# Score passes of a sliding-window attention: the keys' low parts of two head pairs in one matmul

## The chip, the cores and the metric

The kernel runs on one core of one Trainium2 chip. A core has TensorE (matmuls, called PE in the profile, its weight loads PEld), VectorE (DVE), ScalarE (ACT), GpSimd (POOL) and SyncE (SP), which here does nothing but issue DMAs. Each engine works through its own instructions in order and waits on semaphores for the others. The metric is the device time of one execution in microseconds; less is better.

## The reference

One layer of a hybrid decoder block on x of 2048 positions by 1024 channels, all in float32. What matters here is the attention branch: 16 query heads and 4 key/value heads of 64 channels, a window of 128 positions, QK-norm and a sink per head.

```
h = rms_norm(x, norm_g)
u = jnp.einsum('bsd,dc->bsc', h, w_in)      # v_c, b_c, c_c, z_c, q, k, v, z_a, gate_logits
y_a = einsum(b_c * causal_depthwise_conv(c_c * v_c, conv_w) * silu(z_c), w_conv_out)
scores = jnp.einsum('bnqhgd,bnkhd->bnhgqk', qb, kb) * scale     # blocks of 128 queries, 256 keys
p = softmax with sinks over the valid keys (0 <= q_pos - k_pos < 128)
o = einsum(p, vb) * silu(z_a)
y_b = einsum(o, w_attn_out)
out = x + einsum(sigmoid(gates_a) * y_a + sigmoid(gates_b) * y_b, w_out)
```

A position sees itself and the 127 before it, so a block of 64 queries needs 192 keys.

## The kernel before, in words

**Numbers.** TensorE takes float32 operands of a rounded kind (float32r). To keep float32 accuracy every operand is split into a high part (rounded) and a low part (what is left), and a product is a sum of passes: high times high, high times low, low times high.

**Stages.** The sequence is worked through in two tiles of 1024 positions (`t`). In each, "units" run one after the other: k, v, q, the convolution's columns (`cv`, `b`), the gates (`ga`, `gb`), `za`, `z`, and then `ya` and `yb`; at the end of both the output projection `o`. A unit `S` has seven products of 12 passes of 512 columns (`product`, L368). The generators yield after each product, and each yield is a tick: in `run` a tick calls `ahead_loads` (weight loads), then one `piece` of the preparation of the next unit's weights, and whatever was put down for that tick with `put`. The order of every engine is written out in this way; no scheduler changes it.

**Weights.** `load_half` (L246 for the units `S`) brings one half of a unit's raw weights into a tile of `rawpool` with two DMAs on SyncE, up to two units ahead. A unit's pieces then form sums and differences of the raw halves and split them: the pieces "a", "d", sums, "s" and "t", each with a high part copied by ACT (L273) and a low part subtracted by DVE (L274, into tiles called w..al, w..d, w..sl, w..tl). "s" is the last to read the second half, "t" the last to read the first. A raw tile is used again when its last reader has ended, and the DMA that fills it waits for that on SyncE.

**Attention.** While these units run, attention goes along in their ticks: 32 steps for each `t`, one for each key/value head `j` and block `b` of 128 positions (`attention`; the first 16 at every 5.25 ticks, the others at every 3.25). For a step at tick n:

- n - 4: `att_load` brings queries and keys from DRAM: `q2` (L713), for each of the two halves h (64 queries each) and the two head pairs c a 128x128 tile, with the high parts of 64 channels in partitions 0 to 63 and the low parts in 64 to 127; `k2` (L718; L720 and L722 in the first block of a tile), the keys' high parts and low parts of 256 positions, each stored twice over, in partitions 0 to 63 and again in 64 to 127.
- n: `att_scores`. A score tile takes two PSUM banks, one for each h. For each h and c there are two passes (L752) with the weights `q2[:, h, c]`: with the keys' high parts and with the keys' low parts, 192 columns each. Eight passes in all; a pass over the low parts adds low times low as well. The first block of the sequence has 64 or 128 columns, as it has no earlier keys. DVE then masks and takes the maximum (L758 to L764) and forms the biases.
- n + 1: ACT takes the exponentials (`att_exp`, L777); value tiles are loaded (`att_load_v`, L734 and L739).
- n + 2 to n + 8: DVE normalizes, TensorE transposes (L793), ACT, DVE and POOL split and mask (L796 to L806), TensorE multiplies with the values (L823, six passes of 256 columns), ACT and DVE join the halves (`att_out`), and SyncE stores the result to `od` (L836).

There is one score tile (`ps_s`), so a block's scores wait for the exponentials of the block before.

**Queues.** All loads and stores named so far, and the gates' stores (L897), are issued by SyncE, in the program's order: one that waits holds up all behind it. SyncE's transfers take turns with eight semaphores, so that each also waits for the landing of the one eight places ahead of it. POOL's own queue writes the queries, keys and values to DRAM (L609, L698).

Of the kernel before, what the change touches and what calls it, by code (L numbers as in the profile page):

```python
# [8 lines left out]
F32 = mybir.dt.float32  # L9
F32R = mybir.dt.float32r  # L10
# [5 lines left out]
P = 128  # L16
D = 1024
KC = D // P
T = 1024
H = 512  # L20
HB = H // P
NB = T // P
# [3 lines left out]
HD = 64  # L26
# [12 lines left out]
LH, UH = slice(0, HD), slice(HD, P)  # L39
HALVES = (LH, UH)  # L40
# [3 lines left out]
def block_kernel(  # L44
# [15 lines left out]
    nc = tc.nc  # L60
# [5 lines left out]
    consts = ctx.enter_context(tc.tile_pool(name="consts", bufs=1))  # L66
    oppool = ctx.enter_context(tc.tile_pool(name="oppool", bufs=28))
    wpool = ctx.enter_context(tc.tile_pool(name="wpool", bufs=8))
    rawpool = ctx.enter_context(tc.tile_pool(name="rawpool", bufs=5))
    big = ctx.enter_context(tc.tile_pool(name="big", bufs=19))  # L70
    upool = ctx.enter_context(tc.tile_pool(name="upool", bufs=2))
    small = ctx.enter_context(tc.tile_pool(name="small", bufs=12))
# [6 lines left out]
    def slot(shape, dt, name):  # L79
        return big.tile(shape, dt, tag="big", name=name)  # L80
# [7 lines left out]
    def mbank(name):  # L88
# [8 lines left out]
    q2d = [[dram.tile([P, 2 * NB, 2, 2, HD], F32, name=f"q2d{t}_{j}") for j in range(NKV)]  # L97
           for t in range(NT)]
    kd = [dram.tile([NKV, P, 2, T], F32, name=f"kd{t}") for t in range(NT)]
# [113 lines left out]
    def add(o, a, b, eng=None):  # L213
        return (eng or nc.vector).tensor_tensor(out=o, in0=a, in1=b, op=ALU.add)  # L214
# [4 lines left out]
    def mul(o, a, b, eng=None):  # L219
        return (eng or nc.vector).tensor_tensor(out=o, in0=a, in1=b, op=ALU.mult)  # L220


    plan, raws, ready, used, todo = [], {}, [], [0], []
    WRING, RAWS = 8, 5
    live, rawlive = [0], [0]

    def load_half(i=None, first=None):
# [478 lines left out]

    def att_load(t, j, b):
        nm = f"{t}_{j}_{b}"  # L710
        gb = t * NB + b
        q2 = slot([P, 2, 2, P], F32R, f"q2_{nm}")
        nc.sync.dma_start(  # L713
            q2.bitcast(F32).rearrange("p h c x -> p (h c x)"),
            q2d[t][j][:, 2 * b : 2 * b + 2].rearrange("p h c e x -> p (h c e x)"))
        k2 = slot([P, 2, 2 * P], F32R, f"k2_{nm}")
        if b > 0:
            nc.sync.dma_start(k2.bitcast(F32), kd[t][j, :, :, (b - 1) * P : (b + 1) * P])  # L718
        else:
            nc.sync.dma_start(k2[:, :, P:].bitcast(F32), kd[t][j, :, :, 0:P])  # L720
            if gb > 0:
                nc.sync.dma_start(k2[:, :, :P].bitcast(F32), kd[t - 1][j, :, :, T - P : T])  # L722
        return q2, k2

    def att_load_v(t, j, b):

# [15 lines left out]
    def att_scores(t, j, b, ld):  # L742
        first = t * NB + b == 0
        nm = f"{t}_{j}_{b}"
        q2, k2 = ld
        rv = rqs[t, j][:, b // HB, b % HB]
        sp = ps_s.tile([P, 2, 2, 2 * P], F32, tag="s", name=f"s{nm}")
        for h in range(2):
            skip = (2 - h) * HD if first else 0
            for c in range(2):  # L750
                for l in range(2):
                    nc.tensor.matmul(  # L752
                        sp[:, h, c, skip : 3 * HD], lhsT=q2[:, h, c, :],
                        rhs=k2[:, l, h * HD + skip : h * HD + 3 * HD], start=l == 0, stop=l == 1)
        sg = sp.rearrange("p h c k -> p (h c) k")
        m = mask_i.unsqueeze(1).to_broadcast([P, G, HD])
        if first:
            nc.vector.copy_predicated(  # L758
                sg[:, :, 2 * HD : 3 * HD], m, negc.unsqueeze(1).to_broadcast([P, G, HD]))
            nc.vector.tensor_copy(sg[:, 0:2, HD : 2 * HD], negc.unsqueeze(1).to_broadcast([P, 2, HD]))  # L760
        else:
            nc.vector.copy_predicated(sg[:, :, 2 * HD : 3 * HD], m, sg[:, :, 0:HD])
        st = small.tile([P, 6, G], F32, tag="st", name=f"st{nm}")
        nc.vector.tensor_reduce(out=st[:, 0], in_=sg[:, :, HD : 3 * HD], axis=AX.X, op=ALU.max)  # L764
        mul(st[:, 5].rearrange("p (h c) -> p h c", c=2), st[:, 0].rearrange("p (h c) -> p h c", c=2), rv)
        nc.vector.scalar_tensor_tensor(
            out=st[:, 1], in0=st[:, 5], scalar=-1.0, in1=nsink_r[:, j].rearrange("p h c -> p (h c)"),
            op0=ALU.mult, op1=ALU.min)
        add(st[:, 2], sink_r[:, j].rearrange("p h c -> p (h c)"), st[:, 1])
        return sg, st, rv  # L770
# [314 lines left out]
    for n in range(S // P // 2):  # L1085
        t, c0 = divmod(2 * n * P, T)
# [112 lines left out]
    def attention(t, places):  # L1199
        for r, n in enumerate(places):  # L1200
            j, b = divmod(r, NB)
            got = {}

            def step(k, f, got=got):
                def g():
                    got[k] = f(got)
                return g

            put(n - 4, step("l", lambda g, j=j, b=b: att_load(t, j, b)))
            put(n + 1, step("v", lambda g, j=j, b=b: att_load_v(t, j, b)))  # L1210
            put(n, step("s", lambda g, j=j, b=b: att_scores(t, j, b, g["l"])))
            put(n + 1, step("e", lambda g, j=j, b=b: att_exp(t, j, b, g["s"])))
            put(n + 2, step("n", lambda g: att_norm(g["e"])))
            put(n + 4, step("x", lambda g, j=j, b=b: att_turn(t, j, b, g["n"])))
            put(n + 7, step("o", lambda g, j=j, b=b: att_values(t, j, b, g["x"], g["v"])))
            put(n + 8, step("z", lambda g, j=j, b=b: att_out(t, j, b, g["o"])))
# [139 lines left out]
```

## Time and profile before

| | us |
|---|---|
| median of 3 runs | 2016.96 (2016.4 to 2018.07) |
| the profiled execution | 2018.62 |
| its span | 2016.9 |
| TensorE busy in it | 1998.2 |
| score passes (L752), 512 of them, busy | 67.3 |
| their weight loads, busy | 65.6 |
| SyncE's key loads (L718, L720, L722) | 68 transfers |

The granted clock of TensorE was 0.999 of full speed over the span. Matmuls overlap in the profile, as the next one starts before the last has left the array: what a pass takes is the distance between two starts and not the duration shown for one. In the rows of the timeline a piece is a run of equal instructions: start, length, engine, line, operation, tiles written and read, shape and count. A row of an engine's line (say L718) gives the least, median and greatest duration of one instruction; for a DMA that is the time that its issue takes on SyncE, and "DMA to landing" is the time from the issue's start to the landing of its data. Issues on SyncE include a wait, if their time is much longer than others of the same line.

### The profile page before, as it was taken

How to read it: one execution, taken by the hardware profiler on the slowest of the kernel's cores; microseconds unless marked ns; L12 is line 12 of the kernel's file. 1: busy time of each engine (PE TensorE's matmuls, PEld its weight loads, DVE VectorE, ACT ScalarE, POOL GpSimd, SP SyncE). 2: the span in 40 equal slices, each digit the busy share in tenths (PEclk: the TensorE clock that was granted, in tenths of full speed). 3: DMA queues.
4: the chain of work that ended last, by engine and by line, in shares of the span. 5: the costliest groups of instructions: out<-in, count | busy, mean ns of one | idle time of the engine just before them, and what ended most of it. 6: DMA issues, size and time to landing. Idle time of an engine off the chain costs nothing.

```text
span 2016.9 us, 27508 instructions
## 1 busy us (share of the span) xinstructions
PE 1998.2 (99%) x9488; PEld 1664.3 (83%) x9488; DVE 1381.9 (69%) x2361; ACT 933.9 (46%) x1847; POOL 373.3 (19%) x519
## 2 busy tenths in 40 slices
PE   8999999999999999999999999999999999999999
PEld 6788888888888888888888888888888888888887
DVE  6878888787775565358777887886776656356654
ACT  7554554456564343244555454555665334112321
POOL 1462222123230000000272212212322000100000
PEclk9999999999999999999999999999999999999999
DMA  6484443456464535765485434445556444765553
GB/s 181 126 206 121 131 122 104 123 151 184 149 173 157 193 105 159 237 204 163 119 208 153 121 94 124 132 139 157 168 173 185 145 142 136 250 217 165 172 172 110
DMA packets 315707, 316.18 MB, mean 157 GB/s; under 512 B 21564, under 2 KB 235632, under 8 KB 315568
## 3 DMA queue, kind: packets, MB, share of 16 engines
q1 hardware_dynamic: 302528, 276.37, 45.2%
q0 software_dynamic: 13024, 38.06, 7.3%
q8 instruction: 75, 1.23, 0.3%
q14 instruction: 64, 0.52, 0.1%
q10 hardware_dynamic: 16, 0.00, 0.0%
HBM read 217.61 MB, written 96.73 MB: 156 GB/s over the span
## 4 chain that ended last, share of the span: by engine, by line
PE 88%; DVE 5%; ACT 4%; issue 1%; SPq 1%; DMA 1%; ACTq 0%; DVEq 0%
PE Y L368 28%; PE yb L953 9%; PE ya L953 8%; PE Xcv L368 4%; PE Vcv L368 4%; PE s L752 2%; PE Vb L368 2%; PE Xb L368 2%; PE Xza L368 2%; PE Xo L368 2%; PE Xz L368 2%; PE Vz L368 2%; PE Vza L368 2%; PE Vo L368 2%; PE Vq L368 2%; PE po L823 2%
## 5 line engine op out<-in xcount | busy, mean ns | idle before, releaser
L806 POOL TENSOR_SCALAR_AFFINE_SELECT xh<-xh 64x512 fp32r<-64x512 f32 x64 | 67.6, 1056 | 661.9 <-DVE xl L798 536.1
L777 ACT ACTIVATE p<-s,st,rq 128x128 f32<-128x128 f32 x256 | 113.3, 453 | 0.7
L214 DVE TENSOR_TENSOR o<-po,o 64x256 f32<-64x256 f32 x128 | 53.7, 419 | 59.3 <-ACT o L834 59.2
L987 DVE SCALAR_TENSOR_TENSOR tha<-tha,ya 128x512 f32<-128x512 f32 x32 | 22.0, 687 | 94.3 <-PE ya L953 90.9
L834 ACT COPY o<-po 64x256 f32<-64x256 f32 x128 | 46.9, 367 | 85.0 <-DVE o L214 83.5
L798 DVE TENSOR_TENSOR xl<-pt,xh 128x512 fp32r<-128x512 f32 x64 | 44.2, 690 | 57.3 <-ACT yp L797 53.6
L953 PE MATMUL ya<-opa,wya_1h 128*128 128x512 f32 x256 | 79.7, 391 | 1.0 <-ACT opa L210 0.5
L368 PE MATMUL Xcv<-oph,wcv_ah 128*128 128x512 f32 x256 | 79.7, 393 | 0.0
L953 PE MATMUL yb<-opb,wyb_0h 128*128 128x512 f32 x256 | 79.5, 392 | 0.0
L953 PE MATMUL yb<-opb,wyb_1h 128*128 128x512 f32 x256 | 79.5, 392 | 0.0
L953 PE MATMUL ya<-opa,wya_0h 128*128 128x512 f32 x256 | 78.9, 390 | 0.0
L752 PEld LDWEIGHTS s<-k,q 128*128 128x128 f32 x512 | 65.6, 191 | 8.9 <-ACT p L777 5.3
L210 ACT CAST opb<-ocr 128x512 fp32r<-128x512 f32 x32 | 19.9, 621 | 110.4 <-DMA ocr<-ocd 109.2
L752 PE MATMUL s<-k,q 128*128 128x192 f32 (+2 forms) x512 | 67.3, 274 | 2.7 <-ACT p L777 2.5
L1007 DVE SCALAR_TENSOR_TENSOR thb<-thb,yb 128x512 f32<-128x512 f32 x32 | 21.9, 686 | 55.2 <-PE yb L953 55.2
L953 PEld LDWEIGHTS ya<-opa,wya_1h 128*128 128x128 f32 x256 | 48.1, 188 | 12.3 <-ACT opa L210 1.4
L698 POOL DMA_DIRECT2D vd<-v x32 | 20.2, 637 | 199.6 <-DVE v L211 197.3
L953 PEld LDWEIGHTS ya<-opa,wya_0h 128*128 128x128 f32 x256 | 48.1, 188 | 10.0
L953 PEld LDWEIGHTS yb<-opb,wyb_1h 128*128 128x128 f32 x256 | 47.6, 188 | 9.6
L953 PEld LDWEIGHTS yb<-opb,wyb_0h 128*128 128x128 f32 x256 | 47.6, 188 | 9.6
L368 PEld LDWEIGHTS Xcv<-oph,wcv_ah 128*128 128x128 f32 x256 | 47.0, 188 | 9.0
L806 POOL TENSOR_SCALAR_AFFINE_SELECT yp<-xl 64x512 fp32r<-64x512 f32 x64 | 53.5, 836 | 3.1
(583 smaller groups left out, 6202.8 us busy)
## 6 DMA issues: line engine op xcount, KB each, us to landing
wcv_raw<-in_w_in SPq DMA_DIRECT2D x64, 256.0 KB, 4.3
q<-q2d SPq DMA_DIRECT2D x64, 256.0 KB, 4.0
v<-vd SPq DMA_DIRECT2D x128, 128.0 KB, 3.9
gd<-th SPq DMA_DIRECT2D x64, 256.0 KB, 2.1
k<-kd SPq DMA_DIRECT2D x56, 256.0 KB, 4.3
wq_raw<-in_w_in SPq DMA_DIRECT2D x32, 256.0 KB, 4.4
q2d<-q_h POOLq DMA_DIRECT2D x64, 128.0 KB, 3.9
q2d<-q_l POOLq DMA_DIRECT2D x64, 128.0 KB, 4.1
```

The source lines that it names most:

```text
L214: return (eng or nc.vector).tensor_tensor(out=o, in0=a, in1=b, op=ALU.add)
L368: nc.tensor.matmul(ps, lhsT=w[:, j, :], rhs=b[:, m, :], start=start and j == 0 and i == 0, stop=j == KP - 1 and i == 2, skip_group_check=n ...
L698: nc.gpsimd.dma_start(to, v[half].bitcast(F32).rearrange("p b l d -> p b (l d)"))
L752: nc.tensor.matmul(sp[:, h, c, skip : 3 * HD], lhsT=q2[:, h, c, :], rhs=k2[:, l, h * HD + skip : h * HD + 3 * HD], start=l == 0, stop=l == 1)
L777: nc.scalar.activation(out=p[:, i, :], in_=sg[:, i, HD : 3 * HD], func=AF.Exp, bias=st[:, 1, i : i + 1], scale=rv[:, i // 2, i % 2 : i % 2 ...
L798: nc.vector.tensor_tensor(out=xl, in0=pt, in1=xh.bitcast(F32), op=ALU.subtract)
L806: nc.gpsimd.affine_select(out=d4, in_=s4, pattern=[[0, 2 * G], [-sg, HD]], compare_op=ALU.is_gt if prev else ALU.is_ge, fill=0.0, base=0, ...
L823: nc.tensor.matmul(po[:, cs], lhsT=v2[:, kind, :], rhs=xx.rearrange("p g q -> p (g q)")[:, cs], start=n == 0, stop=n == 2)
L834: nc.scalar.copy(ov, pov[oth, :, :, e, :])
L953: nc.tensor.matmul(ps, lhsT=w[:, j, cs], rhs=o[:, m, :], start=n == 0 and i == 0, stop=n == KC - 1 and i == 2)
L987: nc.vector.scalar_tensor_tensor(out=m, in0=m, scalar=1.0, in1=ps, op0=ALU.add, op1=ALU.mult)
L1007: nc.vector.scalar_tensor_tensor(out=m, in0=m, scalar=1.0, in1=ps, op0=ALU.add, op1=ALU.mult)
```

## The change

The products of the queries' high parts with the keys' low parts are taken for both head pairs of a half in one pass, and low times low is no longer computed. The weights of that pass hold the high parts of the queries of pair 0 in partitions 0 to 63 and of pair 1 in partitions 64 to 127. The moving operand has 384 columns: the low parts of 192 keys in partitions 0 to 63 with zeros under them, and beside them the same keys' low parts in partitions 64 to 127 with zeros above. So each pair meets its keys in its own 192 columns. For each h there are then three passes: one of 384 columns into both pairs' places, and one of 192 for each pair with the weights `q2` as before and the keys' high parts, added to it.

The moving operands with the zeros stand in two lasting tiles, `lows`, used by turns; POOL fills them with zeros once, and loads write only the parts with keys. A second tile, `kq`, takes the place of `k2`: it holds the keys' high parts and the weights of the new pass. `lows` takes 4 KB of each partition; the raw weight tiles are cut from five to four (4 KB each). `att_load` issues six transfers in place of two (in the first block of the second tile nine in place of three). The order of everything else on all engines is the same.

```diff
-    rawpool = ctx.enter_context(tc.tile_pool(name="rawpool", bufs=5))
+    rawpool = ctx.enter_context(tc.tile_pool(name="rawpool", bufs=4))
...
-    WRING, RAWS = 8, 5
+    WRING, RAWS = 8, 4
...
+    lows = [consts.tile([P, 2, 2 * P], F32R, name=f"lows{i}") for i in range(2)]
+    for kz in lows:
+        nc.gpsimd.memset(kz.bitcast(F32), 0.0)
+
     def att_load(t, j, b):
...
+        kz = lows[(j * NB + b) % 2]
         q2 = slot([P, 2, 2, P], F32R, f"q2_{nm}")
...
-        k2 = slot([P, 2, 2 * P], F32R, f"k2_{nm}")
-        if b > 0:
-            nc.sync.dma_start(k2.bitcast(F32), kd[t][j, :, :, (b - 1) * P : (b + 1) * P])
-        else:
-            nc.sync.dma_start(k2[:, :, P:].bitcast(F32), kd[t][j, :, :, 0:P])
-            if gb > 0:
-                nc.sync.dma_start(k2[:, :, :P].bitcast(F32), kd[t - 1][j, :, :, T - P : T])
-        return q2, k2
+        kq = slot([P, 2, 2 * P], F32R, f"kq_{nm}")
+        for c in range(2):
+            nc.sync.dma_start(
+                kq[HALVES[c], 1].bitcast(F32).rearrange("p (h x) -> p h x", h=2),
+                q2d[t][j][LH, 2 * b : 2 * b + 2, c].rearrange("p h e x -> p h (e x)"))
+
+        blocks = [(t, b - 1, 0, 2)] if b else [(t, 0, 1, 1)]
+        if b == 0 and gb > 0:
+            blocks.append((t - 1, NB - 1, 0, 1))
+        for kt, k0, to, n in blocks:
+            here, there = slice(to * P, (to + n) * P), slice(k0 * P, (k0 + n) * P)
+            nc.sync.dma_start(kq[:, 0, here].bitcast(F32), kd[kt][j, :, 0, there])
+            for c in range(2):
+                nc.sync.dma_start(kz[HALVES[c], c, here].bitcast(F32), kd[kt][j, HALVES[c], 1, there])
+        return q2, kq, kz
...
         for h in range(2):
             skip = (2 - h) * HD if first else 0
+            keys = slice(h * HD + skip, (h + 3) * HD)
+            nc.tensor.matmul(
+                sp[:, h, :, skip : 3 * HD], lhsT=kq[:, 1, h * P : (h + 1) * P], rhs=kz[:, :, keys],
+                start=True, stop=False)
             for c in range(2):
-                for l in range(2):
-                    nc.tensor.matmul(
-                        sp[:, h, c, skip : 3 * HD], lhsT=q2[:, h, c, :],
-                        rhs=k2[:, l, h * HD + skip : h * HD + 3 * HD], start=l == 0, stop=l == 1)
+                nc.tensor.matmul(
+                    sp[:, h, c, skip : 3 * HD], lhsT=q2[:, h, c, :], rhs=kq[:, 0, keys],
+                    start=False, stop=c == 1)
```

More of the change, by code (lines that the diff above doesn't have):

```diff
@@ L744, in att_scores @@
         nm = f"{t}_{j}_{b}"
-        q2, k2 = ld
+        q2, kq, kz = ld
         rv = rqs[t, j][:, b // HB, b % HB]
```

## The prediction

> **What bounds the kernel now.** I read the page's shares and its chain first, then the chain of waits over a few microseconds of attention, then the timelines of TensorE and of SyncE's queue around single score blocks.
>
> ```profile
> span 2016.9 us, 27508 instructions
> PE 1998.2 (99%) x9488; PEld 1664.3 (83%) x9488; DVE 1381.9 (69%) x2361; ACT 933.9 (46%) x1847; POOL 373.3 (19%) x519
> PE 88%; DVE 5%; ACT 4%; issue 1%; SPq 1%; DMA 1%; ACTq 0%; DVEq 0%
> ```
>
> TensorE is busy for 99% of the span and carries 88% of the chain. So a shorter pass pays one for one, as long as nothing that TensorE waits for comes later. The prices of passes come from the merged chain (start, length up to the next piece, count) and, for the narrow ones, from the timeline of TensorE:
>
> ```profile
> 435.99 0.23 PE Xga L368
> 436.21 0.87 PE s L752 x8
> 437.08 2.76 PE Y L368 x12
> 439.84 0.71 PE po L823 x6
> 440.55 0.44 PE pt L793 x4
> ...
> 303.83 1.00 PE L752 MATMUL s<-k,q 128*128 128x64 f32 x8
> 304.67 0.69 PE L368 MATMUL Y<-oph,wcv_th 128*128 128x512 f32 x2
> ```
>
> Per pass that is 0.87/8 = 0.109 us at 192 columns, 2.76/12 = 0.230 at 512, 0.71/6 = 0.118 at 256 and 0.44/4 = 0.110 at 128. The last two rows are a first block of a sequence, whose eight passes have 64 and 128 columns: from 303.83 to 304.67 is 0.84 us, or 0.105 each. So from 64 to 192 columns a pass costs the same: what it costs is its weight load, which the next pass must wait for. From 256 on the columns cost. A score block of eight loads is bound by loads, and this is what the change touches.
>
> **The change, part by part.**
>
> *Fewer passes.* Each half of a score block had four passes of 192 columns; it gets one of 384 and two of 192. Columns stay at 768, loads fall from four to three. No 384-column pass is in the trace. Its bounds are the 256-column pass (0.118) and the 512-column one (0.230); it lies halfway, so I take 0.174. A block then costs 2 x 0.174 + 4 x 0.109 = 0.784 us, 0.086 less than 0.87; 60 blocks give 5.2 us. The four first blocks have passes of 128, 64, 64 and 256, 128, 128 columns: 5 x 0.105 + 0.118 = 0.64 against 0.84, 0.8 us for four. The gain is 6.0 us. At the ends it would be 0.20 us a block (12.7 us in all) with 0.118, and with 0.230 a loss of 0.026 us a block, 0.8 us in all after the first blocks' gain.
>
> The Trainium skill, TensorE: Matmul & The Clock Gate, Back-to-back issue gap, gives a warm pass N/2.4 + 2.5 ns; by columns alone, a half would cost 332.5 ns before (four of 192) and 327.5 after, an estimate of no gain (0.6 us in 60 blocks). The rows above speak against that rule here, since 64 and 192 columns cost the same; the same page's LDWEIGHTS section gives P/1.2 ns, 107 for 128 columns, with which the 0.109 agrees.
>
> *More waits on TensorE.* The six loads of a block need more wait instructions: two or three ahead of its first pass, where one or two stood, and one between the 384-column pass and the next. The wait ahead of the block at 436.21 cost nothing (the row before it ends where it starts). I take nothing, as the issuer has 0.17 us of the long pass to cover one; uncovered they would be about 0.05 us a block, 3 us.
>
> *More transfers on SyncE.* A block's q and k transfers become six (nine in place of three where a sequence's tile crosses into the next): q2 as before, two of the queries' high parts (64 partitions), one of the keys' high parts, two of their low parts (64 partitions). What an issue costs and when keys land:
>
> ```profile
> L718 SPq DMA_DIRECT2D k<-kd x56: 532/537/1588, 174.7 to 1505.1; - x56
> L739 SPq DMA_DIRECT2D v<-vd x64: 588/591/1800, 170.9 to 1518.5; - x64
> L713 SPq DMA_DIRECT2D q<-q2d x64: 325/522/1303, 144.3 to 1504.4; - x64
> DMA to landing us min/median/max: 3.1/4.3/6.9
> ```
>
> The last row belongs to the first. By the nearest rows the new five are 2 x 0.55 (between the k and v rows) + 0.52 (q) + 2 x 0.47 (v's first issue at 207.63, below) = 2.56 us in place of 0.54: the last keys of a block are issued 2.0 us later. Bounds: five of 0.33 (the least in the q row), 1.1 us later, and five of 0.59, 2.4 us later. The 64 blocks add some 130 us of issues to a queue that is idle or waiting for most of the attention; they are paid only where keys land late. Everything behind them on SyncE (weights, od, yd and gd stores, value loads) slips as much; weights are loaded a whole unit ahead, seven products of 2.76 us, which covers it.
>
> *Four raw tiles.* At most four are ever live, so what is loaded ahead and the order of work stay the same on every engine; the fifth only spares a wait. Now the first half of a pair is loaded into a spare tile and the second half waits for the last reader of the "s" piece (the DVE subtraction into w..sl). With four tiles the first half waits for that, and the second for the last reader of the "t" piece. SyncE issues in order, so value, query and key loads stand behind that wait. An example, the pair ahead of the block at 219.79 (SyncE, then DVE, then TensorE):
>
> ```profile
> 200.71 6.75 SPq L246 DMA_DIRECT2D wcv_raw<-in_w_in  x4
> 207.63 0.47 SPq L734 DMA_DIRECT2D v<-vd  x1
> 208.16 0.59 SPq L739 DMA_DIRECT2D v<-vd  x1
> 208.86 1.30 SPq L713 DMA_DIRECT2D q<-q2d  x1
> 210.27 0.53 SPq L718 DMA_DIRECT2D k<-kd  x1
> ...
> 205.27 1.22 DVE L274 TENSOR_TENSOR wb_sl<-wb_raw,wb_sh 128x1024 fp32r<-128x1024 f32 x1
> 209.09 1.21 DVE L274 TENSOR_TENSOR wb_tl<-wb_raw,wb_th 128x1024 fp32r<-128x1024 f32 x1
> ...
> 219.79 1.03 PE L752 MATMUL s<-k,q 128*128 128x192 f32 x8
> ```
>
> The wait ends at 209.09 + 1.21 = 210.30 in place of 205.27 + 1.22 = 206.49: 3.8 us later. With 2.0 us of issues the last key transfer starts near 210.27 + 5.8 = 216.1 and lands, by the median 4.3, at 220.4: 0.6 us after its block wants it, where it had 5.2 us to spare. Three other blocks are near the edge:
>
> ```profile
> 526.67 2.24 SPq L246 DMA_DIRECT2D wgb_raw<-in_w_in  x4
> 529.57 0.54 SPq L718 DMA_DIRECT2D k<-kd  x1
> 536.67 1.03 PE L752 MATMUL s<-k,q 128*128 128x192 f32 x8
> ...
> 553.81 0.54 SPq L718 DMA_DIRECT2D k<-kd  x1
> 561.60 1.12 PE L752 MATMUL s<-k,q 128*128 128x192 f32 x8
> ...
> 1280.77 1.37 SPq L718 DMA_DIRECT2D k<-kd  x1
> 1290.68 1.03 PE L752 MATMUL s<-k,q 128*128 128x192 f32 x8
> ```
>
> From issue to use they have 7.1, 7.8 and 9.9 us; less 2.0 for issues and the 4.3 they keep 0.8, 1.5 and 3.6, and a landing of 6.9 makes the first two late by 1.8 and 1.1. I take four such blocks late by 0.6 us each, 2.4 us given back. At the ends none is late, or about every fourth block, 16, is.
>
> *Where TensorE waits for DVE and ACT.* In the dense parts of attention it already does (430 to 600 us, then 1345 to 1525):
>
> ```profile
> PE Vgb L368 <- DVE wgb_sl L274: 1.5, 1, 1.5
> PE s L752 <- ACT p L777: 1.4, 2, 1.2
> ...
> PE pt L793 <- DVE p L220: 1.8, 1, 1.8
> PE s L752 <- ACT p L777: 1.1, 2, 0.7
> ```
>
> There a shorter score block only waits longer. Some 26 blocks lie up to the last of these waits, 26 x 0.086 = 2.2 us; DVE's and ACT's chains themselves start from the scores, so I take a quarter as lost, 0.6 us (bounds 0 and 2.2).
>
> *The memsets.* Two more of POOL's 128x512 fills:
>
> ```profile
> 2.06 0.52 POOL L130 MEMSET zero<- 128x512 f32 x1
> 8.30 0.19 POOL L148 COPY seen<-x 128x1 f32<-128x1 f32 x1 [5.73 <-DMA x<-in_x]
> ```
>
> 1.04 us lies in the 5.73 us in which POOL waits for x: nothing.
>
> **The sum.** -6.0 + 2.4 + 0.6 = -3.0 us. The profiled execution took 2018.62 us, its span and 1.7 us around it, and would be 2015.6; against the runs' median of 2016.96, 1.7 us below it, the forecast is 2014.0 us.
>
> **The rivals.** *The queue decides (slower).* SyncE's lateness, not TensorE, sets the attention. For it: the blocks above, where a key transfer has 0.6 to 3.6 us left, and 6.9 us landings that happen already. Against it: most blocks are not right behind a raw pair. With 16 blocks late by 0.75 us it gives 12 - 6.0 + 0.6 = +6.6, 2023.6 us; it turns the sign from nine blocks of 0.6 us on (5.4 us). *All hidden.* Landings stay near 3.1 to 4.3 us, the small transfers land sooner, and only the 0.6 us is lost: -5.4, 2011.6 us. For it: medians that leave room in all but one of the four blocks. *No gain from TensorE.* The 384-column pass costs as much as 512 (0.230): +0.8, and with the late blocks +2.4 it is 2020.2 us; against it stands the evenly rising price between 256 and 512 columns. The skill page's columns-alone rule is this rival too.
>
> **How the numbers follow.** Forecast 0.42, all hidden 0.18, the queue 0.30, no gain 0.10. Within 0.2% (4.0 us; about what a measurement of this kernel can tell from no change) lies most of the forecast. The side faster by over 4.0 takes all hidden and a third of the forecast (its stalls may be half as long): 0.18 + 0.15 = 0.33. Slower by over 4.0 takes the queue but for a tenth, plus a little of no gain: 0.30. The rest is 0.37. The range: below, all hidden with a slightly cheaper pass, 2010.5; above, the queue rival at its middle and a little over, 2025. The forecast's own range is 2011.5 to 2016.5.
>
> **What would show it.** Of the changed kernel: a full score block (passes at L765 and L769) from first pass to the next product in 0.78 us; the weight loads of the score down from 512 to 384; a block behind a raw pair waiting for kq or lows for about half a microsecond, four or so in all; SyncE's waits at L246 naming w..tl beside w..sl; waits for DVE and ACT in the dense parts slightly longer. Wrong would be: a block of 0.87 us or more (the pass's price), waits for keys in ten blocks and more (the queue), or none at all (all hidden).

## The result and the profile after

The changed kernel takes 2013.72 us (median of 22 runs, 2012.46 to 2015.92), the kernel before 2017.32 (22 runs, 2016.35 to 2019.41): a ratio of 0.9982, 95% interval 0.9976 to 0.9988. The forecast was 2014.0. The time came out nearly as forecast; the working did not.

The profiled execution took 2012.82 us. From its page, first the span and the shares, then the chain by engine:

```profile
span 2011.1 us, 27717 instructions
...
PE 1992.2 (99%) x9360; PEld 1656.5 (82%) x9360; DVE 1383.4 (69%) x2361; ACT 934.0 (46%) x1847; POOL 375.3 (19%) x521
...
PE 90%; DVE 4%; ACT 3%; issue 2%; DMA 1%; POOL 0%; SPq 0%; POOLq 0%; ACTq 0%; DVEq 0%
```

TensorE still bounds the kernel, with 128 matmuls and as many weight loads fewer. The score block whose chain the prediction quoted (436.21 us before) looks like this after, in the merged chain of the same place (start, length, count):

```profile
435.14 0.17 PE s L765
435.31 0.20 PE s L769 x2
435.51 0.20 PE s L765
435.71 0.20 PE s L769 x2
435.91 2.81 PE Y L368 x12
```

The block takes 0.77 us in place of 0.87. But the twelve passes of 512 columns behind it, which the change does not touch, take 2.81 us in place of 2.76. Over the 15 full blocks between 1098 and 1343 us the medians of the block are 0.871 before and 0.766 after, the means of the twelve passes 2.756 and 2.807: 0.105 gained, 0.051 lost again, 0.053 us kept (3.627 to 3.574 for both together). From the thirteenth pass on there is no difference. A first block of a sequence, in TensorE's timeline:

```profile
303.58 0.22 PE L765 MATMUL s<-lows,kq 128*128 128x128 f32 x1
...
304.20 0.68 PE L368 MATMUL Y<-oph,wcv_th 128*128 128x512 f32 x2
```

From 303.58 to 304.20 it takes 0.62 us in place of 0.84. What TensorE waits for (sum, times, longest), rows with scores, transposes and the gates' weights, first before, then after:

```profile
PE s L752 <- ACT p L777: 2.5, 4, 1.2
PE pt L793 <- DVE p L220: 2.2, 2, 1.8
...
PE Vgb L368 <- DVE wgb_sl L274: 1.5, 1, 1.5
```

```profile
PE s L765 <- ACT p L794: 3.2, 6, 1.3
...
PE pt L810 <- DVE p L220: 2.3, 2, 1.8
...
PE Vgb L368 <- DVE wgb_sl L274: 1.1, 1, 1.1
...
PE Vga L368 <- DVE wga_sl L274: 0.2, 1, 0.2
```

No row of this view after the change has a DMA in it: no score block waited for `kq` or `lows`. The waits shown grew by 0.6 us (3.2 + 2.3 + 1.1 + 0.2 against 2.5 + 2.2 + 1.5).

So the measured sum is 60 x 0.053 = 3.2 us from the full blocks and 4 x 0.22 = 0.9 from the first ones: -4.1 us, against -3.6 between the medians, whose interval reaches from 2.4 to 4.8. The two profiled spans are 5.8 us apart. Some 1.7 us of that is a stretch of slower clock that the profiled execution before had and the one after had not; these rows give TensorE's granted clock behind the count of POOL, before and after:

```profile
1380.00:1400.00 20.00, 18.12 (x85) 14.85 (x84) 12.87 (x26) 11.09 (x24) 6.22 (x8) 0.91 0.53 163
```

```profile
1380.00:1400.00 20.00, 18.05 (x86) 14.73 (x85) 13.24 (x25) 13.81 (x35) 6.22 (x8) 1.00 0.55 164
```

The score blocks of the changed kernel are 3.38 us earlier than those before up to the block ahead of this stretch, and 5.07 us behind it. Such a step is not what the change gains: 13 of the 89 executions of the kernel before that were timed beside the experiments have a mean granted clock of 0.999 or less, and 7 of the 22 of the changed kernel.

The 0.6 us of longer waits does not show as a loss. From the first score block to the last, and without that stretch, the changed kernel draws ahead of the kernel before by 4.3 us, and of two more traces with the eight passes (four_raw and six_transfers, below) by 3.8 and 4.5 us. The blocks between give 4.0 without any loss: 59 x 0.053 + 4 x 0.22.

### The profile page after: what moved, and what is told of

Its sections match the earlier page's. It is cut to its first block, busy times and chain, and to the rows that moved or that the text cites. A ratio compares the mean times of both kernels' runs of the same rounds, so it can differ in the third digit from the quotient of the medians.

```text
span 2011.1 us, 27717 instructions
## 1 busy us (share of the span) xinstructions
PE 1992.2 (99%) x9360; PEld 1656.5 (82%) x9360; DVE 1383.4 (69%) x2361; ACT 934.0 (46%) x1847; POOL 375.3 (19%) x521
## 4 chain that ended last, share of the span: by engine, by line
PE 90%; DVE 4%; ACT 3%; issue 2%; DMA 1%; POOL 0%; SPq 0%; POOLq 0%; ACTq 0%; DVEq 0%
PE Y L368 28%; PE yb L970 9%; PE ya L970 8%; PE Xcv L368 4%; PE Vcv L368 4%; PE Vb L368 2%; PE Xb L368 2%; PE Xza L368 2%; PE Vz L368 2%; PE Vo L368 2%; PE Xz L368 2%; PE Xo L368 2%; PE Vza L368 2%; PE po L840 2%; PE Vq L368 2%; PE Xq L368 2%
## 5 line engine op out<-in xcount | busy, mean ns | idle before, releaser
L889 DVE SCALAR_TENSOR_TENSOR y<-u,cols,y 128x512 f32<-128x512 f32 x64 | 49.1, 767 | 6.2 <-ACT y L882 5.0
L813 ACT CAST xh<-pt 128x512 fp32r<-128x512 f32 x64 | 37.4, 585 | 33.4 <-PE pt L810 32.2
```

Source lines behind the costliest of these rows:

```text
L813: nc.scalar.copy(xh, pt)
L889: nc.vector.scalar_tensor_tensor(out=y, in0=u[:, h * H + i : h * H + i + H], scalar=tap(i, k), in1=y, op0=ALU.mult, op1=ALU.add)
```

## The experiments

**The raw tile alone and the transfers alone.** Two edits of the kernel before, each with one of the two parts that the prediction charged to SyncE. The first has only four raw tiles:

```diff
-    rawpool = ctx.enter_context(tc.tile_pool(name="rawpool", bufs=5))
+    rawpool = ctx.enter_context(tc.tile_pool(name="rawpool", bufs=4))
...
-    WRING, RAWS = 8, 5
+    WRING, RAWS = 8, 4
```

> The kernel before with four raw weight tiles in place of five and nothing else. If the longer wait of SyncE behind a raw pair is covered, as the changed kernel's profile suggests (no score block waited for a key there): within 1 us of before, 2016.5 to 2018.5. If the queue's lateness costs something that the shorter passes paid for in the changed kernel: 2 us or more above before, 2019.3 and up.

Measured: 2017.64 us (2016.77 to 2018.81), ratio to before 1.0002, interval 0.9993 to 1.001. The fifth tile was worth nothing that can be measured.

The second keeps five raw tiles and the eight old passes, and splits the two transfers of a block into six:

```diff
+        for h, rs in ((0, slice(0, P)), (1, LH), (1, UH)):
+            nc.sync.dma_start(
+                q2[rs, h].bitcast(F32).rearrange("p c x -> p (c x)"),
+                q2d[t][j][rs, 2 * b + h].rearrange("p c e x -> p (c e x)"))
...
+            for l, rs in ((0, slice(0, P)), (1, LH), (1, UH)):
+                nc.sync.dma_start(k2[rs, l, here].bitcast(F32), kd[kt][j, rs, l, there])
```

> The kernel before, five raw tiles, its eight passes and the same tiles and bytes, but the queries and keys of a block come in six transfers (nine where a tile crosses into the next), three for the queries and three for the keys, as many as in the changed kernel. In the changed kernel the twelve passes of 512 columns behind a score block take 231.5 ns each in place of 227, some 0.05 us a block that eats half of what the block saves. If the extra waits on TensorE for six transfers make that (the issue theory): the same slower passes here, and 64 x 0.05 = +3.3 us, 2020.6 us. If the new passes make it (the pass theory): passes behind the block at 227 to 228 and a time within 1 us of before.

Measured: 2017.61 us, ratio 1.0001, interval 0.9991 to 1.001. In its chain the block costs what it did and starts where the piece before it ends (1123.23 + 2.77 = 1126.00), so neither the issues nor the additional waits on TensorE cost anything:

```profile
1123.23 2.77 PE Vb L368 x12
1126.00 0.87 PE s L754 x8
```

**The new passes without the new transfers.** The changed kernel with two transfers per block:

```diff
-        for c in range(2):
-            nc.sync.dma_start(
-                kq[HALVES[c], 1].bitcast(F32).rearrange("p (h x) -> p h x", h=2),
-                q2d[t][j][LH, 2 * b : 2 * b + 2, c].rearrange("p h e x -> p h (e x)"))
...
-                nc.sync.dma_start(kz[HALVES[c], c, here].bitcast(F32), kd[kt][j, HALVES[c], 1, there])
+        if b > 0:
+            nc.sync.dma_start(kq.bitcast(F32), kd[t][j, :, :, (b - 1) * P : (b + 1) * P])
...
```

> The changed kernel (384-column passes, four raw tiles) with two transfers a block as before: q2, and the keys' high and low parts as they stand into kq. It leaves out the loading of the tiles with the zeros, which stay zero, and the queries in kq, so the low passes run on the wrong numbers; the passes, their count and columns are those of the change. Issue theory: score blocks of 0.77 us, passes behind them back at 227, and a gain of 64 x 0.105 = 6.7 less about 0.6 lost to DVE and ACT: 2011.2 us. Pass theory: passes behind the block still at 231 or so and the changed kernel's time, 2013.7 us, within 0.7.

Measured: 2013.53 us (2012.94 to 2014.57), ratio 0.9981, interval 0.9972 to 0.999: the changed kernel's time, with the changed kernel's block and, behind it, its long twelve passes:

```profile
1123.57 0.17 PE s L760
...
1124.34 2.81 PE Y L368 x12
```

So all of the gain, and the loss behind the block too, belongs to the passes: neither their data (the lows stay zero here) nor the transfers have to do with it.

**The order of the passes.** The lengthening behind the block was not expected, so its dependence on the order was tried. In the first of these runs the wide pass of each half goes last:

```diff
-            nc.tensor.matmul(
-                sp[:, h, :, skip : 3 * HD], lhsT=kq[:, 1, h * P : (h + 1) * P], rhs=kz[:, :, keys],
-                start=True, stop=False)
             for c in range(2):
                 nc.tensor.matmul(
                     sp[:, h, c, skip : 3 * HD], lhsT=q2[:, h, c, :], rhs=kq[:, 0, keys],
-                    start=False, stop=c == 1)
+                    start=c == 0, stop=False)
+            nc.tensor.matmul(
+                sp[:, h, :, skip : 3 * HD], lhsT=kq[:, 1, h * P : (h + 1) * P], rhs=kz[:, :, keys],
+                start=False, stop=True)
```

> The changed kernel with the 384-column pass last in each half instead of first: the two passes with the keys' high parts come first. Six transfers and the same number of waits. Issue theory: the same slow passes behind the block, time within 0.7 us of 2013.7. Pass theory: the last pass before the product is now a long one under which the product's first weight load is hidden; the first passes behind the block come at 227 to 230, and the time falls by up to 3.3 us, to 2010.5.

Measured: 2012.24 us (2011.63 to 2014.62), ratio 0.9978, interval 0.9969 to 0.9987. The issue theory is out with this. The time falls by 1.5 us and not by 3.3, as the block is longer (0.80 us); the twelve passes behind it are shorter than in either kernel:

```profile
1123.53 0.20 PE s L766 x2
1123.73 0.20 PE s L769
1123.93 0.20 PE s L766 x2
1124.13 0.20 PE s L769
1124.34 2.74 PE Y L368 x12
```

The remaining orders write the six passes from a list of (half, what), where 0 and 1 are a pair's narrow pass and 2 is the wide one. Each kernel has one of these lists:

```diff
-        for h in range(2):
+        order = ((0, 0), (0, 1), (0, 2), (1, 2), (1, 0), (1, 1))
+        order = ((0, 2), (0, 0), (0, 1), (1, 0), (1, 1), (1, 2))
+        order = ((1, 0), (0, 2), (0, 0), (1, 1), (1, 2), (0, 1))
+        order = ((0, 2), (1, 2), (0, 0), (1, 0), (0, 1), (1, 1))
+        order = ((0, 2), (1, 2), (0, 0), (0, 1), (1, 0), (1, 1))
+        for h, c in order:
```

The lists, from the first to the last, are those of lows_adjacent, lows_outside, lows_spread (and spread_again), wide_first_mixed and wide_first_grouped; after_again is the changed kernel as it is.

> The six score passes of the changed kernel in another order: the first half's 384-column pass last in its half, the second half's first, so that the two wide passes stand side by side and the block still ends with two narrow passes behind a wide one (narrow, narrow, wide, wide, narrow, narrow). Theory A (the twelve passes behind a block are lengthened by how the block ends): they take 2.81 us as in the changed kernel, and with a block of about 0.79 us (0.086 + 0.113 + 0.203 + 0.195 + 0.087 + 0.113) the kernel takes 2014 to 2015 us. Theory B (they are lengthened by wide passes standing ahead of narrow ones anywhere in the block, in proportion): about 2.78 us, and 2013 us. Theory C (it is the number of the score's passes or their loads): 2.81 us for any order, which the run with the wide passes last, 2.74 us, already speaks against.

> The six passes in the order wide, narrow, narrow, narrow, narrow, wide. Theory A: the block ends with a wide pass, so the twelve passes behind it take 2.74 us as with both wide passes last; block about 0.80 us (0.171 + 0.089 + 3 x 0.112 + 0.203); 2012.2 us. Theory B: one half of two is in the changed kernel's order, so the passes take about 2.78 us and the kernel 2013.5 us.

> The six passes of the two halves mixed so that only two narrow ones are neighbours: narrow, wide, narrow, narrow, wide, narrow. A narrow pass behind a wide one took 0.087 us, one behind a narrow one 0.113, a wide one behind a narrow one 0.195 to 0.203: block 0.086 + 0.200 + 0.088 + 0.112 + 0.200 + 0.087 = 0.773 us. Theory A with one narrow pass at the end being harmless: passes behind it 2.75 us, 2011 us or a little below, the fastest of all orders. Theory A with any narrow end behind a wide pass being harmful: 2.80 us and 2013.5 us. If the block and the passes behind it together are what counts and the array only shifts time from one to the other, their sum is near 3.55 us as with the wide passes last, 2012.2 us.

> What counts is the block and the twelve passes behind it together: before 3.627 us, after 3.574, wide passes last 3.546, side by side 3.546, outside 3.554, spread 3.513. Twelve passes at 0.227 leave 0.790 us for the spread order, which is four narrow passes at 0.112 and two wide ones at 0.170. The other orders carry 0.06 us on top for two places where a wide pass is followed by both narrow passes of one half (the changed kernel), 0.03 to 0.04 for one such place (last, side by side, outside), nothing for none (spread). Here: both wide passes first, then the narrow ones of the two halves by turns. Theory (the place costs because two narrow passes into the same half follow a wide one): nothing on top, 3.51 us, the kernel at 2011 to 2012.4 us as with the spread order. Rival (it costs wherever two narrow passes follow a wide one, whatever half they write): 0.03 us or more on top, 3.545 us, 2012 to 2013 us.

> The same with the narrow passes of the first half ahead of those of the second: wide, wide, narrow and narrow of the first half, narrow and narrow of the second. Theory (two narrow passes into the same half behind a wide one): one such place, 3.545 us for the block and the twelve passes, 0.035 more than with the halves by turns. Rival (whatever half they write): the same 3.545 us in both orders. If both are at 3.51 the place has nothing to do with it.

> The changed kernel as it is, beside the spread order on the same chip: block and twelve passes 3.574 us, 2013.7 us.

> The spread order once more, beside the changed kernel on the same chip: block and twelve passes 3.513 us. If all of the 0.061 us a block is kept, 64 blocks give 3.9 us and the kernel is at 2009.8 us; by the first runs of it, 2012.4 against 2013.7, about 1.5 us are kept, and the rest is lost in places where TensorE waits for ACT or DVE anyway or where a block stands in front of other than twelve wide passes.

What came out, all in us; block and twelve passes over the same 15 blocks as above, N a narrow pass and W a wide one:

| kernel | order | block | twelve behind | both | time | ratio to before |
|---|---|---|---|---|---|---|
| before | NNNNNNNN | 0.871 | 2.756 | 3.627 | 2017.32 | |
| changed | WNN WNN | 0.766 | 2.807 | 3.574 | 2013.72 | 0.9982 |
| after_again | WNN WNN | 0.766 | 2.807 | 3.573 | 2014.56 | 0.9985 |
| low_last | NNW NNW | 0.803 | 2.743 | 3.546 | 2012.24 | 0.9978 |
| lows_adjacent | NNW WNN | 0.773 | 2.773 | 3.546 | 2011.88 | 0.9976 |
| lows_outside | WNN NNW | 0.793 | 2.761 | 3.554 | 2012.92 | 0.9979 |
| lows_spread | N W N N W N | 0.766 | 2.747 | 3.513 | 2012.40 | 0.9976 |
| spread_again | N W N N W N | 0.766 | 2.748 | 3.514 | 2012.42 | 0.9975 |
| wide_first_mixed | WW NNNN | 0.771 | 2.776 | 3.547 | 2012.92 | 0.9978 |
| wide_first_grouped | WW NNNN | 0.771 | 2.775 | 3.546 | 2012.33 | 0.9976 |

The chains of two of them, lows_adjacent and lows_spread:

```profile
1122.60 0.20 PE s L776 x2
1122.80 0.37 PE s L772 x2
1123.17 0.20 PE s L776 x2
1123.37 2.77 PE Y L368 x12
```

```profile
1122.42 0.09 PE s L776
1122.50 0.20 PE s L772
1122.70 0.20 PE s L776 x2
1122.90 0.20 PE s L772
1123.10 0.09 PE s L776
1123.18 2.75 PE Y L368 x12
```

Theory A (how the block ends) falls with lows_adjacent: it ends like the changed kernel, and the passes behind it take 2.77 and not 2.81. Theory B's 2.78 for half of the order is near that one, but not the 2.76 of lows_outside. The next theory, that two narrow passes into the same half cost something behind a wide one, falls too: wide_first_mixed and wide_first_grouped agree to 0.001 us. Its rival foresaw that, but would have the spread order, where a wide pass is also followed by two narrow ones, at 3.545 and not at 3.513. So the order changes the time of the block and the passes behind it by up to 0.06 us, and each trace shows the same value block after block, but no rule that was tried foretells all orders, and what makes passes of 512 columns take longer than 0.227 us for a while stays open.

The spread order beside the changed kernel on one chip: 2012.42 (2011.15 to 2014.04) against 2014.56 (2013.07 to 2015.3), ratios to before 0.9975 (0.9966 to 0.9984) and 0.9985 (0.9977 to 0.9994). It is the fastest by its trace. By the runs it and lows_adjacent cannot be told apart, and its interval still overlaps that of the changed kernel. The 0.061 us a block would be 3.9 us over 64 blocks; 1.3 to 2.1 us showed up. In the dense parts, where TensorE waits for ACT, the traces of lows_spread and of the changed kernel hardly draw apart: over the blocks between 469 and 590 us the lead of the spread order falls from 0.62 to 0.41 us, and over those between 1374 and 1510 us it only grows from 1.57 to 1.68, while in the other parts it grows by 0.06 a block.

**One tick less for the loads.** The changed kernel with `att_load` three ticks ahead of the scores:

```diff
-            put(n - 4, step("l", lambda g, j=j, b=b: att_load(t, j, b)))
+            put(n - 3, step("l", lambda g, j=j, b=b: att_load(t, j, b)))
```

> The changed kernel with queries and keys of each step loaded one tick later, three ticks ahead of its scores in place of four. In the trace of the changed kernel the last transfer of a block lands 0.56 us ahead of its first score pass at the least, and 19 of 64 blocks have less than a product of 2.8 us to spare. Theory (nothing was late because landings are short, and the cover is nearly used up): these 19 blocks now wait on TensorE for kq or lows, by 21 us in all at most if every microsecond of it is a stall of its own, about 15 us if later blocks profit from the stalls of earlier ones: 2025 to 2035 us. Rival (the cover is far larger than the queue's times show, as what holds the queue at the tick before is gone a tick later): no waits for keys, 2014 us.

Measured: 2033.58 us (2027.4 to 2037.17), ratio 1.0078, interval 1.0066 to 1.009. TensorE's waits now name the keys, and the first row of the view is new:

```profile
PE s L765 <- DMA lows<-kd: 9.1, 8, 1.9
PE s L765 <- ACT p L794: 2.7, 5, 1.2
```

Set beside the changed kernel's trace, the shift of the score blocks grows at 13 of them, by 0.3 to 2.4 us each and 20 us in all, and none of it is made good later. The named waits are less than this, as some of the same stalls stand under other names, and as only some 16 us of the 20 are waits. About 3.4 us are two stretches of slower clock behind such waits, which the changed kernel's trace does not have (the clock is 0.91 behind the count of POOL, as above):

```profile
235.00:255.00 20.00, 18.19 (x78) 14.89 (x77) 11.53 (x21) 7.83 (x18) 3.63 (x4) 0.91 0.35 95
375.00:395.00 20.00, 18.08 (x80) 14.91 (x79) 12.28 (x22) 7.57 (x18) 2.11 (x2) 0.91 0.26 76
```

The time is in the expected range, but not by the blocks that were counted: 7 of the 13 are among the nineteen, and the other twelve of those lost nothing. Some of the twelve stand behind a raw pair, whose wait holds their loads either way: at the block at 219.77 the first of them is issued 7.1 to 7.2 us ahead of the block in both kernels. So the rival's reason holds for these, and the theory's for the others. The cover was real, and at 12 blocks less than a tick wide.

## Why the prediction was right, and where it was not

The time (2014.0 against 2013.72) was right by luck: one term was 1.2 us too small, one of 2.4 us never came, one of 3.1 us nobody had counted, and what was left of these errors was nearly made up by the kernel before, whose median of 22 runs is 2017.32 and not the 2016.96 that the forecast started from. Forecast were 3.0 us less, measured 3.6.

*Fewer passes: right in kind, too small.* The forecast block was 0.784 us, a gain of 0.086; it is 0.766, a gain of 0.105. The wide pass itself was priced about right: 0.171 us behind a pass of 512 columns and 0.195 behind a narrow one, mean 0.183, against 0.174. The error lies with the narrow passes, which stayed at 0.109 in the sum. Behind a wide pass one takes 0.087 us (from its start to the next, median), and only the one after it 0.113. The trace before had this already: of its eight passes the first, behind one of 512 columns, takes 0.086 and the other seven 0.110 to 0.116, and the mean of 0.109 hid it. The changed block has two such first passes. The first blocks were right: 0.62 against a forecast of 0.64. In all this term was -7.2 us (60 x 0.105 + 0.9) and not -6.0. The rival of no gain from TensorE is out, and with it the columns-alone reading of the Trainium skill's TensorE: Matmul & The Clock Gate, Back-to-back issue gap. Four passes of 192 columns are 330.0 ns by it and not the 332.5 of the prediction, so its estimate is 0.005 us a block (0.3 us in 60), and the trace shows 0.105. That section of the Trainium skill itself calls the formula the gap of an isolated matmul, which counts too little at small widths in a stream with a weight load for each pass; the trace agrees, with 0.109 us against 0.0825 for 192 columns.

*The passes behind the block: the step that was missing.* The prediction let the gain end with the block. 0.051 us of each 0.105 goes back in the next twelve passes, 60 x 0.051 = 3.1 us. It comes with the new passes alone (two_transfers has it, six_transfers has not), and it depends on their order.

*More waits on TensorE: right.* Taken as nothing; six_transfers has them and loses nothing.

*Transfers and raw tiles: the queue as forecast, the landing not.* SyncE after the change, at the example of the prediction:

```profile
206.59 4.71 SPq L246 DMA_DIRECT2D wcv_raw<-in_w_in  x4
211.40 0.45 SPq L748 DMA_DIRECT2D v<-vd  x1
...
213.25 1.25 SPq L725 DMA_DIRECT2D kq<-q2d  x2
214.55 0.59 SPq L734 DMA_DIRECT2D kq<-kd  x1
215.18 1.10 SPq L736 DMA_DIRECT2D lows<-kd  x2
```

The value load that was issued at 207.63 goes at 211.40, 3.8 us later, as worked out from the wait for w..tl. The last key transfer starts at 215.18 + 0.55 = 215.7; the forecast was 216.1. SyncE's waits name the new partner too (both rows are from the trace after, for the unit cv; the view before has no row for wcv_tl):

```profile
SPq L246 <- DVE wcv_sl L274: 44.9, 9, 16.5
...
SPq L246 <- DVE wcv_tl L274: 9.1, 9, 1.7
```

But the landing had been taken from the old transfer's 4.3 us. From the view of DMAs (number, KB each, median us from issue to landing):

```profile
q<-q2d SPq DMA_DIRECT2D x64, 256.0 KB, 4.1
...
kq<-q2d SPq DMA_DIRECT2D x128, 64.0 KB, 4.0
...
kq<-kd SPq DMA_DIRECT2D x56, 128.0 KB, 3.4
lows<-kd SPq DMA_DIRECT2D x112, 64.0 KB, 2.8
```

The size alone does not make a landing short: the queries' pieces of 64 KB take 4.0 us, the keys' of 64 KB 2.8. In the order of their issue the six take 4.0, 4.0, 3.8, 3.3, 3.0 and 2.6 us (medians over the full blocks), so the keys of a block are there 6.0 us after its first issue, where the two old transfers took 4.8. The last issue itself comes 2.5 us later than before behind the first (3.1 in place of 0.6), more than the 2.0 of the forecast. Why the later ones land sooner was not tried.

In the example the last transfer lands 2.6 us after its issue, at 218.3, 1.5 us ahead of its block at 219.77 where the forecast had it 0.6 late. The three other blocks that the prediction quoted held as well: in the whole trace the closest landing is 0.56 us ahead of its block. So the 2.4 us for four late blocks is the step that failed, and its mis-sized term is the 4.3 us, for which the trace has 2.6 for the last transfer of a block. The prediction had itself written that no waits for keys at all would speak for "all hidden", and in that respect this rival was the true case; its 2011.6 us missed, as it lacked the loss behind the blocks. The queue rival was wrong here by one tick: load_late pays 20 us, 16 of them in waits.

*DVE and ACT in the dense parts: not seen.* The named waits grew by the 0.6 us of the forecast, but the starts of the score blocks show no such loss: the changed kernel draws ahead by 3.8 to 4.5 us, where the blocks alone give 4.0 and a loss of 0.6 would leave 3.4. Three traces do not tell 0.6 us from nothing with certainty.

*The memsets: right.* Two of them in 0.98 us, and POOL's wait for x shrinks by nearly as much, to 4.85 us from 5.73:

```profile
2.52 0.98 POOL L712 MEMSET lows<- 128x512 f32 x2
8.36 0.19 POOL L148 COPY seen<-x 128x1 f32<-128x1 f32 x1 [4.85 <-DMA x<-in_x]
```

The forecast's sum was -6.0 + 2.4 + 0.6 = -3.0; by the traces it is -7.2 + 3.1 = -4.1.

## What to carry to other kernels

When passes are merged to save weight loads, measure the stretch from the first of them to well behind the last: here half the gain of a block was given back in the twelve wide passes after it, and only the sum of both agrees with the kernel's time. Several orders of the same passes are then worth a run each; mixing narrow and wide passes was shortest here by the traces (3.513 us against 3.574), while the runs cannot tell it from lows_adjacent. Price a pass by its place and not by the mean of a group: the first narrow pass behind a wide one was cheaper than the rest, in the trace before as well. When a transfer is split into several, do not add the old landing to the last issue: here the last was issued 2.5 us later behind a block's first, and the keys were there only 1.2 us later (6.0 us in place of 4.8).

## What the runs showed of the hardware beyond that

A pass of 192 columns takes 0.087 us behind one of 384 and 0.113 behind another of 192. That the wide pass hides more than the next weight load cannot be read from this: behind the wide pass that starts at 1122.80 in the trace after, the loads of the two narrow passes begin at 1122.80 and 1122.97, and the passes themselves start at 1122.97 and 1123.06. So one load begins under the wide pass, and the second with the first narrow pass. A stream of 512-column passes at 0.227 us each runs at 0.224 to 0.240, 0.232 on average, from the second to the eleventh pass behind the changed kernel's block, with the granted clock at 1.00 over those 245 us. Six transfers in place of two, and the waits that go with them, cost TensorE nothing while they land ahead of use. Where keys came too late (load_late), none of the time was made good, and behind two of the stalls 20 us with a granted clock of 0.91 came on top.
